# Strassen's scheme for one half of an output projection, on one Trainium2 core

## The chip, the cores and the metric

The kernel runs on one core of a Trainium2 chip. TensorE (PE) multiplies matrices and loads its stationary operand in a sub-stream of its own (PEld); VectorE (DVE), ScalarE (ACT) and GpSimd (POOL) do elementwise work; SyncE (SP) issues nearly all transfers, which run on 16 DMA engines. Each engine takes its instructions in order, and they synchronize by semaphores. The metric is the device time of one execution in microseconds. The kernel before took 450.61 us, the median of three runs (448.91 to 451.24).

## The reference

One encoder layer on 1024 tokens of width 1024: a combined input projection, two groups of attention heads, a gate on each, an output projection, and a LayerNorm over residual and projection.

```python
h = jnp.einsum('bsd,de->bse', x, w_in[layer])
q_a, k_a, v_a, z_a, q_b, k_b, v_b, z_b = jnp.split(h, SPLIT_POINTS, axis=-1)
y_a = neighborhood_attention(...)            # 8 heads, 8 x 16 window on a 16 x 64 grid
y_b = windowed_gqa_with_sink(...)            # 8 query heads, 2 key heads, |i - j| <= 128, rotary
mixed = jnp.concatenate([y_a * jax.nn.silu(z_a), y_b * jax.nn.silu(z_b)], axis=-1)
y = jnp.einsum('bse,ed->bsd', mixed, w_out[layer])
x = layer_norm(DEEPNORM_ALPHA * x + y, ln_gain[layer], ln_bias[layer])
```

All inputs are float32. The change concerns `y = mixed @ w_out`, a 1024 x 1024 x 1024 product, and what prepares its operands.

## The kernel before

**Precision.** Each float32 operand of a large product is split into two float16 parts, h (rounded) and l (the rest), after a scale by a power of two. A product is then three matmuls: h*h, h*l and l*h, added up in PSUM. A split is a cast on ACT (the h part) and, for l, one operation on DVE or two on POOL: scale (`L975`), subtract (`L976`).

**Stages.** First the values and the first six column blocks of the input projection. Then the attention: 128 units (group, head pair, head, block of 128 queries), the 'b' heads first. In one unit PE multiplies queries by keys (`stage_qk`, L799 and L800), DVE adds bias or mask and takes the row minimum of the negated scores (L809), ACT exponentiates (L823), ACT and DVE split the result (L831, L832), a DMA transposes it (L835), and PE multiplies it by the values one group of four units at a time (`stage_pv`, L861), some nine units later. `stage_on` normalizes, `stage_ot` transposes on PE (L882) and multiplies by the gate (L885, L888) into `zt[e]`, one tile of 128 mixed channels by 1024 tokens for each e from 0 to 7. The 'b' heads are e = 4 to 7, and come first.

**What fills PE.** Between these steps PE runs the rest of the input projection (`project`, L381): a list of matmuls is handed out by `pump_to`, so many for each unit (`FILL_AT`, `FILL_N`). The last of that filler, 60 matmuls, belongs to the output projection already (`out_head`).

**What sets the order.** Inside the attention the order on each engine is the order in which a Python loop over units writes it (`manual_schedule`). Work on the side is put into queues of `Op` for act, dve, pool and sp; in each unit `pop` emits a fixed number of those whose predecessors were emitted earlier. After the loop `ordered.close()` ends the manual order, and `final()` is ordered by the scheduler of the framework.

**PSUM.** Eight banks of 128 x 512 float32: two with tag `pj` (groups of the projection), four with `s` (scores), two with `t`. A bank can be written again once its readers are done.

**Output projection.** `mixed` is the stationary operand by tiles of 128 tokens, `wo` the moving one by halves of 512 columns. `out_mms(t, a, ps, es)` (L1008) adds the products of row tile t and column half a over the depth blocks `es` into one bank. `wo` is loaded by pieces of 256 KB, twice for six of them: once to take its size (`wo_scan`), once to split it (`wo_split`). Eight of the 16 pieces are split in the attention, eight in `final()`; the parts of `mixed` are made for e = 4 to 7 in the attention (`m_queue`, L990 and L991), for e = 0 to 3 in `final()` (`m_split`, L915, L916).

**End of the layer.** `residual` (L1054, L1057) adds a bank to the tile of x and collects statistics; `norm` finishes a row tile: aggregate (L1061), square root on ACT (L1063), reciprocal (L1068), then half of the columns on DVE and half on ACT and POOL (L1102 to L1108), and stores. The last half tile is computed in pieces of 256, 128 and 128 columns, and `norm_last` finishes it.

Of the kernel before, what the change touches and what calls it, by code (L numbers as in the profile page):

```python
# [25 lines left out]
MSCALE = 2.0 ** -44  # L26
QSCALE = 2.0 ** -15
LTT, LPP, BH, ND, NA, NX, F1 = 1, 6, 9, 1, 1, 6, 0.2
# [14 lines left out]
WO_TAG = ("wor", "wor", "raw", "raw") + ("wr",) * 5 + ("wor", "wor", "raw", "raw", "raw", "wr", "wr")  # L43
WO_SCAN = ((9, 2), (12, 4), (10, 6), (13, 8), (14, 10), (15, 13))
WO_PREV = {15: ("s", 9), 0: ("s", 10), 1: ("s", 15), 2: ("s", 12), 3: ("s", 13), 11: ("s", 14)}
WO_SCALE = 55
M_AT = [105, 112, 118, 120]
WO_AT = [67, 71, 75, 79, 84, 88, 93, 98]
WO_LD = [16, 22, 19, 25, 36, 39, 42, 45, 48, 112, 116, 28, 130, 130, 130, 130]
# [7 lines left out]
def hybrid_block(ctx, tc, xT, x, wt, wv, wo, bias, sink, gain, lbias, cos, sin, bmask, out):  # L57
# [15 lines left out]
    vd = dram.tile([4, GW, ROWS, 4 * VE], F16, name="vd")  # L73

# [29 lines left out]
    wos = const.tile([128, 1], F32, name="wos")  # L104
    yc = const.tile([128, 1], F32, name="yc")
# [30 lines left out]
    ENG = ("act", "dve", "pool", "sp")  # L136
# [3 lines left out]
    class Op:  # L140
        def __init__(self, eng, fn, deps, prio):
            self.eng, self.fn, self.deps, self.step = eng, fn, [d for d in deps if d is not None], None
            self.prio, self.born, self.lag = prio, clock["step"], 2 if eng == "sp" else 0

        def emit(self):
            self.fn()
            self.step = -1 if clock["step"] is None else clock["step"]

    def enq(eng, fn, *deps, prio=1, after=0):
        op = Op(eng, fn, deps, prio)  # L150
        if clock["step"] is not None:
            queues[eng].append(op)
        elif after:
            events.setdefault(ran[0] + after, []).append(op.emit)
        else:
            op.emit()
        return op

    ran, events = [0], {}

# [7 lines left out]

    def need(*ops):
        for op in ops:  # L170
            if op.step is None:
                need(*op.deps)
                queues[op.eng].remove(op)
                op.emit()
# [10 lines left out]
    def w_split(m):  # L185
# [18 lines left out]
        o = enq("act", hi, load_ops.get(("w", m)), prio=0.5)  # L204
        o = enq("pool", lo, o, prio=0.5)
# [80 lines left out]
    def split_k(p, half, src, dep=None):  # L286
# [4 lines left out]
        for j in range(2):  # L291
# [5 lines left out]
            def dup_(w, j=j, a=a, o=o):  # L297
# [6 lines left out]
            dup = [enq("pool", lambda d=dup_: d("kh"), o1, after=32 if dep else 0),  # L304
                   enq("pool", lambda d=dup_: d("kl"), o2, after=36 if dep else 0)]
# [101 lines left out]
    with ExitStack() as vctx:  # L407
# [26 lines left out]
        def load_wv(k, cuts=(0, 640)):  # L434
# [4 lines left out]
            h = vw.tile([128, 640], F32R, name=f"wvh{k}")  # L439
            l = vw.tile([128, 640], F32R, name=f"wvl{k}")  # L440
# [9 lines left out]
        def first_tiles():  # L450
            xr = vp.tile([128, 512], F32, tag="xr", name="xraw", bufs=4)
            wr = wv_stage(0)
            h = vw.tile([128, 640], F32R, name="wvh0")
            l = vw.tile([128, 640], F32R, name="wvl0")
# [271 lines left out]
    rawp = ctx.enter_context(tc.tile_pool(name="rawp", bufs=3, reuse_waits="tile"))  # L726
    actx = ExitStack()
    tiles["kq"] = actx.enter_context(tc.tile_pool(name="kq", bufs=4, reuse_waits="tile"))
    ap = actx.enter_context(tc.tile_pool(name="ap", bufs=3, reuse_waits="tile"))
    tiles["ap"] = ap  # L730


# [46 lines left out]
    def stage_qk(u):  # L779
# [12 lines left out]
        else:  # L792
# [5 lines left out]
            init = nsk[:, h:h + 1]  # L798
        nc.tensor.matmul(ps[:, :n], q, sl[0], start=True, stop=False)  # L799
# [15 lines left out]
    def stage_exp(u):  # L815
        m = 128 * geom(u)[1] + (u[0] == "b")
        sn, nm = st.pop((u, "sn")), st.pop((u, "nm"))
# [8 lines left out]
    def stage_tr(u):  # L826
        n, m = geom(u)
        pt = st.pop((u, "p"))
        hl = split[units.index(u) % NSPLIT]
        src = pt[:, :128 * m].rearrange("p (k c) -> p k c", c=128)  # L830
# [32 lines left out]
    def stage_on(q):  # L863
        g, p, j, h = quad(q)
        ps = st.pop((q, "o"))
        ri = ap.tile([128, 4], F32, tag="ri", name="ri", bufs=4)
        w = VE if g == "a" else HD
# [6 lines left out]
    def stage_ot(q):  # L874
# [4 lines left out]
        ps = bank("t")  # L879
        o = on.pop((g, p, h))  # L880
# [12 lines left out]
    FILL_N = [48] * len(FILL) + [9, 9, 6, 12, 24]  # L893
# [10 lines left out]
    mh, ml = {}, {}  # L904
    EO = (4, 5, 6, 7, 0, 1, 2, 3)

    def m_alloc(e):
        if e >= 4:
            t = big_tile(f"m{e}", (128, 2, S), F16)
        else:  # L910
            t = tiles["fp"].tile([128, 2, S], F16, tag="m", name=f"m{e}", bufs=4)
        mh[e], ml[e] = t[:, 0, :], t[:, 1, :]

    def m_split(e, sl, hi, lo):
        hi(mh[e][:, sl], zt[e][:, sl])  # L915
        lo(ml[e][:, sl], zt[e][:, sl], mh[e][:, sl])  # L916

    WO_SEQ = [(e, a) for a in range(2) for e in EO[:4]] + [(e, a) for e in EO[4:] for a in range(2)]
    wo_parts = {}

    wo_raw = {}

    def wo_load(n, scan=False):
        tag = ("wor" if n in (9, 10, 15) else "raw") if scan else WO_TAG[n]
        pool, bufs = (rawp, 3) if tag == "raw" else (wp, {"wr": 5, "wor": 2}[tag])
        raw = pool.tile([128, 512], F32, tag=tag, name=f"wor{n}", bufs=bufs)
        e, a = WO_SEQ[n]
        nc.sync.dma_start(raw, wo[e, :, 512 * a:512 * a + 512])
        wo_raw[("s", n) if scan else n] = raw

    wo_ops = {}

    def wo_scan(n, scan=False):
        def act():
            raw = wo_raw.pop(("s", n))
            nc.scalar.activation(raw, raw, AF.Abs, accum_out=wom[:, n:n + 1])

        def dve():
            nc.vector.tensor_reduce(wom[:, n:n + 1], wo_raw[n], axis=mybir.AxisListType.X, op=ALU.add,
                                    apply_absolute_value=True)  # L940

        load = load_ops["wo", ("s", n) if scan else n]
        wo_ops["s", n] = enq("act", act, load) if scan else enq("dve", dve, load)

    def wo_scale():
        need(*[wo_ops["s", n] for n in range(16)])
        ps = bank("t")
        nc.tensor.matmul(ps[:, :16], ones, wom.bitcast(BF16)[:, 1::2], start=True, stop=True)
        nc.vector.tensor_reduce(wog, ps[:, :16], axis=mybir.AxisListType.X, op=ALU.max)
        nc.vector.tensor_scalar_max(wog, wog, 2.0 ** -30)  # L950
        nc.vector.tensor_scalar(wog.bitcast(I32), wog.bitcast(I32), 0x7F800000, None, op0=ALU.bitwise_and)
        nc.vector.tensor_scalar(wos.bitcast(I32), wog.bitcast(I32), 0x7F800000, None, op0=ALU.bitwise_xor)
        nc.vector.tensor_scalar(yc, wog, mc, 1.0, op0=ALU.mult, op1=ALU.mult)

    def wo_split(n):
        def hi():
            if n % 2 == 0:
                if n < 8:
                    t = big_tile(f"wo{n}", (128, 2, 2, 512), F16)
                else:  # L960
                    t = tiles["fp"].tile([128, 2, 2, 512], F16, tag="wo", name=f"wo{n}", bufs=4)
                for i in range(2):
                    wo_parts[n + i] = [t[:, i, 0, :], t[:, i, 1, :]]
            if hi_eng == "act":
                nc.scalar.activation(wo_parts[n][0], wo_raw[n], AF.Copy, scale=wos)
            else:
                nc.vector.tensor_scalar_mul(wo_parts[n][0], wo_raw[n], wos)

        def lo():
            h, l = wo_parts[n]  # L970
            raw = wo_raw.pop(n)
            if q == "dve":
                nc.vector.scalar_tensor_tensor(l, raw, wos, h, op0=ALU.mult, op1=ALU.subtract)
            else:
                nc.gpsimd.tensor_scalar(raw, raw, wos, 1.0, op0=ALU.mult, op1=ALU.mult)  # L975
                nc.gpsimd.tensor_sub(l, raw, h)  # L976

        q = "dve" if n in (2, 5, 8, 9, 10, 11, 14) else "pool"
        hi_eng = "act" if clock["step"] is not None or WO_SEQ[n][1] == 1 else "dve"
        o = enq(hi_eng, hi, load_ops.get(("wo", n)))  # L980
        o = enq(q, lo, o)
        wo_ops[n] = o

    m_ops = {}

    def m_queue(e):
        m_alloc(e)
        m_ops[e] = []
        for h in (slice(0, 512), slice(512, S)):
            o = enq("act", lambda h=h: nc.scalar.copy(mh[e][:, h], zt[e][:, h]))  # L990
            m_ops[e].append(enq("pool", lambda h=h: nc.gpsimd.tensor_sub(  # L991
                ml[e][:, h], zt[e][:, h], mh[e][:, h]), o))
# [5 lines left out]
    def out_mms(t, a, ps, es, c=(0, 512)):  # L998
        o, w = c
        ts, cs = slice(128 * t, 128 * t + 128), slice(o, o + w)  # L1000
        ps = ps[:, o:o + w]
        for e in es:
            n = WO_SEQ.index((e, a))
            if n in wo_ops:
                need(wo_ops[n], *m_ops.get(e, ()))
            woh, wol = wo_parts[n]
            for i, (lh, rh) in enumerate(((mh[e], woh), (mh[e], wol), (ml[e], woh))):
                nc.tensor.matmul(ps, lh[:, ts], rh[:, cs],  # L1008
                                 start=(e == EO[0] and i == 0), stop=(e == EO[-1] and i == 2))
                yield  # L1010
# [14 lines left out]
    def final():  # L1025
# [5 lines left out]
        for e in EO[4:]:  # L1031
            m_alloc(e)
# [268 lines left out]
```

## Time and profile before

| | |
|---|---|
| Median of three runs | 450.61 us |
| Profiled execution | 447.86 us, of which the span of instructions is 446.1 us |
| PE busy | 438.3 us (98%), 3241 matmuls |
| DVE, ACT, POOL busy | 346.8, 302.6, 211.7 us |
| Last matmul of the output projection | about 439.0 us from the start of the span |
| DMA | 71.20 MB, mean 160 GB/s |

In a row of instruction groups the columns are line, engine, operation, out<-in, shape and count, then busy time in us and the mean duration of one in ns, then the idle time of the engine just before them and what ended it. In a row of a chain or a timeline the first number is the start in us from the start of the span, the second the length. A row of waits has the waiting engine and line, the one that released it, then the total in us, how often, and the longest. "DMA to landing", and the last number of a DMA issue, is the time from issue until the data is there. Matmuls overlap, so the distance between two starts says more than the duration of one.

### The profile page before, as it was taken

To read this page: it belongs to the slowest core of one execution; us is meant where nothing else is said; L and a number is where in the kernel's file an instruction comes from. 1 tells how busy PE (TensorE), PEld (TensorE's weight loads), DVE (VectorE), ACT (ScalarE), POOL (GpSimd) and SP (SyncE) were. 2 spreads that over 40 slices of the span, in tenths; PEclk is the share of its full clock that TensorE was granted. 3 is DMA by queue.
4 is the path that set the end of the run, shared out by engine and by line. 5 is a ranking of instruction groups with operands and counts; after the bars stand their busy time and mean duration, and the time that the engine had idled before them with its cause. 6 is when DMAs were issued, how large, how long until landed. Compare 5 with 4: busy or idle time off the path is not lost.

```text
span 446.1 us, 9265 instructions
## 1 busy us (share of the span) xinstructions
PE 438.3 (98%) x3241; PEld 254.7 (57%) x3241; DVE 346.8 (78%) x842; ACT 302.6 (68%) x636; POOL 211.7 (47%) x227
## 2 busy tenths in 40 slices
PE   9999999999999999999999999999999999999995
PEld 8997754444445565655564655555555654444454
DVE  5988867429986797898988887888877737679945
ACT  5849789666599988886867777777777847012411
POOL 0110074636939558767505656655642404304740
PEclk9999999999999999999999999999999999999998
DMA  7921569991149999586876769569569588102711
GB/s 266 391 94 60 164 222 325 278 307 54 48 118 221 188 202 181 95 159 135 168 109 126 144 130 169 112 135 184 116 110 242 108 185 318 48 1 92 238 72 71
DMA packets 123983, 71.20 MB, mean 160 GB/s; under 512 B 96800, under 2 KB 105888, under 8 KB 123936
## 3 DMA queue, kind: packets, MB, share of 16 engines
q1 hardware_dynamic: 123792, 70.48, 65.6%
q8 instruction: 25, 0.41, 0.4%
q14 instruction: 22, 0.18, 0.1%
q10 hardware_dynamic: 144, 0.13, 0.1%
HBM read 41.19 MB, written 6.32 MB: 107 GB/s over the span
## 4 chain that ended last, share of the span: by engine, by line
PE 82%; ACT 5%; DVE 4%; DMA 4%; issue 3%; POOL 1%; SPq 0%; DVEq 0%; POOLq 0%; ACTq 0%
PE ps_pj L381 36%; PE ps_s L1008 9%; PE ps_s L488 6%; PE ps_t L861 6%; PE ps_pj L1008 5%; PE ps_t L1008 5%; PE ps_s L799 3%; PE ps_s L800 3%; PE ps_pj L488 3%; PE ps_t L488 3%; DMA vd<-vt 2%; DMA ws<-in_wt 2%; ACT split L831 1%; PE ps_t L882 1%; DVE qs L257 1%
## 5 line engine op out<-in xcount | busy, mean ns | idle before, releaser
L381 PE MATMUL ps_pj<-xf,wh 128*128 128x512 f16 x672 | 201.3, 379 | 0.9 <-DVE ks L257 0.5
L381 PE MATMUL ps_pj<-xf,wl 128*128 128x512 f16 x336 | 127.3, 379 | 0.0
L381 PEld LDWEIGHTS <-wh 128*128 128x128 f16 x672 | 63.4, 98 | 61.9 <-DVE ks L257 1.3
L823 ACT ACTIVATE ps_s<-sn,nm 128x385 f32<-128x385 f32 (+3 forms) x128 | 70.9, 554 | 29.0 <-DVE nm L809 28.6
L832 DVE SCALAR_TENSOR_TENSOR split<-ps_s,split 128x384 f16<-128x384 f32 (+1 forms) x128 | 66.8, 522 | 30.1 <-ACT split L831 28.4
L1008 PEld LDWEIGHTS <-m 128*128 128x128 f16 x432 | 40.0, 98 | 41.2 <-DVE m L916 0.3
L831 ACT ACTIVATE split<-ps_s 128x384 f16<-128x384 f32 (+1 forms) x128 | 58.6, 458 | 2.4
L381 PEld LDWEIGHTS <-wl 128*128 128x128 f16 x336 | 32.9, 98 | 38.3
L198 POOL TENSOR_SCALAR wr<-wr,wsc 128x512 f32<-128x512 f32 x26 | 20.5, 790 | 66.6 <-ACT wh L193 54.4
L809 DVE CUSTOM_DVE_ANT_0 sn<-ps_s,bm,nsk 128x384 f32<-128x384 f32 (+1 forms) x64 | 40.7, 635 | 0.8 <-PE ps_s L800 0.6
L1008 PE MATMUL ps_s<-wo,m 128*128 128x512 f16 (+1 forms) x192 | 40.7, 366 | 0.0
L799 PE MATMUL ps_s<-ks,qs 128*128 128x384 f16 (+2 forms) x128 | 39.7, 310 | 0.1
L800 PE MATMUL ps_s<-ks,qs 128*128 128x384 f16 (+2 forms) x128 | 39.7, 310 | 0.0
L809 DVE CUSTOM_DVE_ANT_0 sn<-ps_s,bias,sg 128x368 f32<-128x368 f32 (+1 forms) x64 | 36.2, 565 | 3.8 <-PE ps_s L800 3.2
L861 PEld LDWEIGHTS <-tr 128*128 128x128 f16 (+1 forms) x1056 | 36.2, 98 | 2.4
L199 POOL TENSOR_TENSOR wl<-wr,wh 128x512 f16<-128x512 f32 x26 | 32.7, 1256 | 2.2
L299 POOL COPY ks<-ks 64x512 f16<-64x512 f16 x40 | 26.2, 663 | 13.8 <-ACT ks L251 5.2
L1008 PE MATMUL ps_pj<-wo,m 128*128 128x512 f16 (+1 forms) x144 | 26.5, 326 | 0.0
L1107 POOL TENSOR_TENSOR xr<-xr,gb 128x512 f32<-128x512 f32 x7 | 9.8, 1398 | 32.5 <-ACT xr L1104 32.5
L1008 PE MATMUL ps_t<-wo,m 128*128 128x512 f16 x96 | 22.8, 379 | 0.0
L488 PEld LDWEIGHTS <-xf 128*128 128x128 f16 x192 | 18.6, 98 | 7.2
L800 PEld LDWEIGHTS <-qs 128*128 128x128 f16 x128 | 12.5, 98 | 15.5 <-issue 0.8
(190 smaller groups left out, 783.6 us busy)
## 6 DMA issues: line engine op xcount, KB each, us to landing
ws<-in_wt SPq DMA_DIRECT2D x15, 512.0 KB, 6.9
wr<-in_wt SPq DMA_DIRECT2D x26, 256.0 KB, 3.5
wor<-in_wo SPq DMA_DIRECT2D x22, 256.0 KB, 3.3
xr<-in_x SPq DMA_DIRECT2D x8, 512.0 KB, 8.7
out<-xr SPq DMA_DIRECT2D x15, 256.0 KB, 2.0
bias<-in_bias SPq DMA_DIRECT2D x8, 440.0 KB, 3.9
wvraw<-in_wv SPq DMA_DIRECT2D x9, 320.0 KB, 5.8
xraw<-in_xT SPq DMA_DIRECT2D x11, 256.0 KB, 4.4
```

Of the source, the lines that this page charges most:

```text
L199: nc.gpsimd.tensor_sub(l, raw, h)
L299: nc.gpsimd.tensor_copy(place(t, o, half, col), place(t, a, half, col))
L381: nc.tensor.matmul(ps, a[:, k % 4, :], mv, start=(k == 0 and i == 0), stop=(k == KT - 1 and i == 2))
L488: nc.tensor.matmul(ps[:, :320], lh[:, ts], rh[:, cs], start=(k == ko[0] and i == 0), stop=(k == ko[-1] and i == 2))
L799: nc.tensor.matmul(ps[:, :n], q, sl[0], start=True, stop=False)
L800: nc.tensor.matmul(ps[:, :n], q, sl[1], start=False, stop=True)
L809: nc.vector.tensor_tensor_reduce(sn[:, :n], ps[:, :n], bias_t, sg[:, c:c + 1], init, op0=ALU.add, op1=ALU.min, accum_out=nm)
L823: nc.scalar.activation(pt[:, :m], sn[:, :m], AF.Exp, bias=nm, scale=-1.0, accum_out=acc)
L831: nc.scalar.activation(hl[:, :m, 0, :], src, AF.Copy, scale=PSCALE)
L832: nc.vector.scalar_tensor_tensor(hl[:, :m, 1, :], src, PSCALE, hl[:, :m, 0, :], op0=ALU.mult, op1=ALU.subtract)
L861: nc.tensor.matmul(ps[:, w * m:w * m + e], a, b_, start=(i == 0), stop=(i == len(mms) - 1))
L1008: nc.tensor.matmul(ps, lh[:, ts], rh[:, cs], start=(e == EO[0] and i == 0), stop=(e == EO[-1] and i == 2))
```

## The change

The 'b' half of the depth (e = 4 to 7) becomes two pairs of depth blocks. For each pair the product is a 2 x 2 block product: A11, A12, A21, A22 are the halves of 512 tokens by the two depth blocks of `mixed`, B11 to B22 the two depth blocks by column halves of `wo`. Winograd's form of Strassen's scheme computes it with seven block products (q1 to q7 in `TERMS`) instead of eight; it needs four sums S1 to S4 of blocks of `mixed` and four, T1 to T4, of blocks of `wo`. The 'a' half stays as eight. In `final()` row tiles t and 4 + t are worked on together, and a bank is read by DVE and then added into further: q1 goes to C11, with q6 on top to C12, with q7 on top to C22, with p4 on top to C21. So an `add` on DVE stands between matmul groups on the same bank, eight adds for a pair of tiles where there were four.

Around it:

- The sums S are made in float32 in `zt`, the sums T in the loaded tiles of `wo`; then both are split. The split T blocks are stored to DRAM (`td`) and loaded back near the end of the attention.
- `wo` is loaded as four tiles of 1 MB for its size, one of them a second time for the T blocks, and 14 blocks of 256 KB to be split.
- All splits of `wo`, and of `mixed` but for two blocks that depend on the last unit, are in the attention.
- The queues keep books: each step's own work is booked on its engine, an operation may be open to several engines ("any"), and `fill_in` emits one where the planned end of the engine's work lies before the next step.
- `final()` is now inside the manual order; `norm` leaves the columns to ACT and POOL, and four tiles of x are loaded and scaled before it.

```diff
-MSCALE = 2.0 ** -44
+MSCALE = 2.0 ** -46
-    FILL_N = [48] * len(FILL) + [9, 9, 6, 12, 24]
+    FILL_N = [48] * len(FILL) + [12, 12, 6, 15, 18]
...
+    def fill_in(eng):
+        now = at_step(clock["step"])
+        ready = [op for e in (eng, "any") for op in queues[e] if op.prio > 1 and (e == eng or eng in op.cost) and all(
+            d.step is not None and d.step + d.lag < clock["step"] + (d.eng == eng) and (d.eng == eng or d.fin < now)
+            for d in op.deps)]
+        if ready:
+            op = min(ready, key=lambda op: op.prio)
+            queues[op.eng].remove(op)
+            op.emit(eng)
...
+    TERMS = {"q1": [("A11", "B11", n) for n in range(NSP)], "q6": [("S2", "T2", n) for n in range(NSP)],
+             "q5": [("S1", "T1", n) for n in range(NSP)], "q7": [("S3", "T3", n) for n in range(NSP)],
+             "q2": [("A12", "B21", n) for n in range(NSP)] + [(a, b, n) for n in NB for a, b in (("A11", "B11"), ("A12", "B21"))],
+             "q3": [("S4", "B22", n) for n in range(NSP)] + [(a, b, n) for n in NB for a, b in (("A11", "B12"), ("A12", "B22"))],
+             "p4": [("A22", "T4", n) for n in range(NSP)] + [(a, b, n) for n in NB for a, b in (("A21", "B11"), ("A22", "B21"))],
+             "d": [(a, b, n) for n in NB for a, b in (("A21", "B12"), ("A22", "B22"))]}
...
+        for t in range(4):
+            if t == 3:
+                b[3] = run("q1", 3, bank("s"))
+            add(t, 0, b[t])
+            cb = run("q5", t, bank("t" if t < 2 else "s"))
+            run("q6", t, b[t])
+            add(4 + t, 1, cb)
+            if t == 3:
+                add(t, 1, cb)
+            add(t, 1, b[t])
+            if t < 3:
+                run("q2", t, a[t], (5,))
+                add(t, 0, a[t], whole=True)
+            d = run("d", t, bank("pj"))
+            run("q7", t, b[t])
+            add(4 + t, 1, d)
+            add(4 + t, 1, b[t], whole=True)
+            if t < 3:
+                run("q3", t, cb)
+                add(t, 1, cb, whole=True)
+                norm(t)
+            run("p4", t, b[t])
+            add(4 + t, 0, b[t], whole=True)
+            norm(4 + t)
+            for n in ((2, 6), (3, 7), (), ())[t]:
+                x_scale(n)
+        add(3, 0, run("q2", 3, bank("pj")), whole=True)
...
+        if i in T_RD:
+            t_soon((3, 0, 1, 2)[T_RD.index(i)])
+        if i in X_RD:
+            x_soon((0, 4, 1, 5)[X_RD.index(i)])
...
     clock["step"] = None
+    final()
     ordered.close()
-    final()
```

`prod(name, t, ps, ...)` takes the place of `out_mms` and issues three matmuls for each term; `add` takes the place of `residual`.

504 lines of the change are left out of this document (297 added, 207 removed).

## The prediction

> **What bounds the kernel now.** I read the page first, then busy time by stage, then who waits for whom, then the chain that ends last.
>
> ```profile
> span 446.1 us, 9265 instructions
> PE 438.3 (98%) x3241; PEld 254.7 (57%) x3241; DVE 346.8 (78%) x842; ACT 302.6 (68%) x636; POOL 211.7 (47%) x227
> ```
> ```profile
> 122.00:240.00 118.00, 118.00 (x1015) 66.67 (x1014) 99.61 (x282) 97.83 (x249) 72.98 (x73) 1.00 0.81 157
> 240.00:330.00 90.00, 89.01 (x783) 50.74 (x779) 74.13 (x198) 68.85 (x141) 54.66 (x67) 1.00 0.72 136
> 330.00:371.40 41.40, 41.40 (x382) 24.21 (x381) 26.36 (x77) 28.91 (x57) 8.93 (x8) 1.00 0.87 185
> ```
> ```profile
> 371.40:439.00 67.60, 67.60 (x363) 33.27 (x361) 52.66 (x92) 18.44 (x26) 29.09 (x21) 1.00 0.31 113
> ```
>
> Columns of the stages are busy time (and instructions) of PE, PEld, DVE, ACT, POOL, then clock, DMA share, GB/s. The first three are the attention, the fourth the output stage. A busy PE could still be a slow one, so I look at its pace in the chain:
>
> ```profile
> 241.93 0.71 DVE ks L257
> 242.68 1.47 PE ps_pj L381 x6
> ...
> 326.48 0.70 DVE qs L257
> 327.23 0.82 PE ps_pj L381 x3
> ...
> 402.63 5.18 PE ps_t L1008 x24
> ```
>
> 24 matmuls of 512 columns in 5.18 us are 0.216 us each, and the output stage runs at that pace without a hole: matmuls taken out there come off the time one for one, and each new PE wait goes on. In the attention PE loses little, but the rows at 241.93 and 326.48 show it released by a DVE evacuation. There DVE and ACT are nearly as tight as PE (waits from 245 to 325 us):
>
> ```profile
> DVE split L832 <- ACT split L831: 11.0, 19, 0.8
> ACT ps_s L823 <- DVE nm L809: 7.8, 12, 1.1
> ACT qs L251 <- DVE qs L257: 6.0, 6, 1.1
> ACT ks L251 <- DVE ks L257: 4.2, 5, 0.9
> PEld L381 <- DVE ks L257: 0.6, 1, 0.6
> ```
>
> In this stretch DVE and ACT wait for each other and never for PE: both run behind PE and set when PSUM banks come free.
>
> **The change, part by part.** (a) *Matmuls.* Before, the output projection is 8 row tiles x 2 column halves x 8 depth blocks x 3 = 384 products of 512 columns. After, the half of the 'b' heads is 7 products x 2 pairs x 4 tiles x 3 = 168 in place of 192; the other half stays 192. 24 fewer x 0.216 = **-5.2 us**. The last half tile is cut in 256, 128 and 128 columns in both kernels; its share is equal within 0.2 us. In the instruction order 63 of the products lie ahead of the last attention transpose, before it was 72; that only moves the border.
>
> (b) *Hand-offs in the output stage.* Before, a bank is filled once, read once, and PE goes on in another. After, q1's bank is read by DVE, then PE adds q6 into the same bank, DVE reads, q7, DVE reads, p4. PE therefore waits for DVE adds (`add`, one scalar_tensor_tensor each), and this part is now written by hand order. Prices, by form in the output stage:
>
> ```profile
> L1057 DVE BATCH_NORM_STATS2 stats<-xr 128x6 f32<-128x512 f32 x14 | 9.5, 684 | 0.1
> L1054 DVE SCALAR_TENSOR_TENSOR xr<-ps_s,yc,xr 128x512 f32<-128x512 f32 x7 | 5.2, 737 | 5.4 <-PE ps_s L1008 5.4
> L1061 DVE BATCH_NORM_AGGREGATE mv<-stats 128x2 f32<-128x12 f32 x7 | 1.4, 196 | 0.1
> L1068 DVE RECIPROCAL rstd<-sd 128x1 f32<-128x1 f32 x8 | 1.2, 144 | 0.0
> L888 DVE SCALAR_TENSOR_TENSOR z<-ps_t,zc,z 128x512 f32<-128x512 f32 x1 | 0.8, 751 | 3.0 <-PE ps_t L882 3.0
> L1029 DVE MEMSET eps<- 128x1 f32 x1 | 0.1, 59 | 0.0
> ```
> ```profile
> 402.67 0.19 DVE L1061 BATCH_NORM_AGGREGATE mv<-stats 128x2 f32<-128x12 f32 x1
> 402.89 0.29 ACT L1063 ACTIVATE sd<-mv,eps 128x1 f32<-128x1 f32 x1 [2.26 <-DVE mv L1061]
> 436.17 2.84 PE L1008 MATMUL ps_pj<-wo,m 128*128 128x128 f16 x48
> 436.37 0.48 DVE L1054 SCALAR_TENSOR_TENSOR xr<-ps_s,yc,xr 128x256 f32<-128x256 f32 x1 [0.91 <-PE ps_s L1008]
> ```
>
> DVE starts 0.20 us after PE has gone to the next bank (436.17 to 436.37); PE starts 0.04 us after a DVE read (241.93 + 0.71 to 242.68); DVE to ACT and back takes 0.03 to 0.05.
>
> - q6(1) and q6(2): DVE's order between p4 of the tile before and the add that frees q1's bank is add, bn_stats, aggregate, [sqrt on ACT], reciprocal, add: 0.20 + 0.74 + 0.68 + 0.04 + 0.20 + 0.03 + 0.29 + 0.05 + 0.14 + 0.74 + 0.04 = 3.15 us. PE has only q5 meanwhile, 6 x 0.216 = 1.29. Wait 1.86 each, 3.7 together.
> - q6(3): the same chain, but q1(3) and q5(3) cover 2.59: 0.6.
> - q6(0): after the last attention transpose z, the eps memset and the add: 0.20 + 0.75 + 0.06 + 0.74 + 0.04 = 1.79 against 1.29: 0.5.
> - d(0): the pj banks both hold q2 sums begun in the attention, so d(0) waits until q2(0) is read. Two adds after q6(0), 0.20 + 2 x 0.74 + 0.04 = 1.72, less q2's three matmuls 0.65: 1.1.
> - p4(3): q3 was put last, so nothing lies between q7(3) and p4(3): 0.20 + 0.74 + 0.04 = 1.0.
>
> Sum **+6.9 us**. The other reuses have 12 to 18 matmuls (2.6 to 3.9 us) between and cost nothing; without that cover each is again 1.0. Without the 0.24 of hand-off in each of the six it is 5.4; with as much again, 8.3. Behind a waiting PE only its own queue hangs: ACT and DVE have idle time here, and POOL, which now does gain and bias of whole tiles where it did halves, goes from 29.09 us to at most 58 of some 70. The stage's final 7 us (last matmul to the end) do not change.
>
> (c) *Splitting in the attention.* By the order of instructions ACT gets 14 more casts of wo, 12 more of the gated output, and 3 more scans; DVE loses 3 scans and gains some 5 sums or splits, which is even; POOL gains 13 two-step splits, 11 subtracts, 14 sums.
>
> ```profile
> L965 ACT ACTIVATE wo<-wor,wos 128x512 f16<-128x512 f32 x12 | 8.6, 713 | 6.0 <-DMA wor<-in_wo 5.5 <-DMA tr<-split 0.5
> L990 ACT CAST m<-z 128x512 f16<-128x512 f32 x8 | 4.5, 608 | 0.0
> L936 ACT ACTIVATE wor<-wor 128x512 f32<-128x512 f32 x6 | 3.7, 620 | 0.0
> ```
> ```profile
> L976 POOL TENSOR_TENSOR wo<-wor,wo 128x512 f16<-128x512 f32 x6 | 7.0, 1160 | 0.5
> L975 POOL TENSOR_SCALAR wor<-wor,wos 128x512 f32<-128x512 f32 x6 | 4.7, 786 | 0.4
> ```
>
> ACT: 14 x 0.71 + 12 x 0.61 + 3 x 0.62 = 19.1 us on 195.6 of 249.4, 86%. POOL: 13 x 1.95 + 25 x 1.16 = 54 on 136.6, 77%, and no wait of PE on POOL is listed. Room there is, but in order: of ACT's new casts, 6 of wo and 6 of the output (7.9 us) stand among the units that ran from 240 to 330 us. From below this is -1.0, if the new order also ends the waits that PE has there (90.00 less 89.01); from above all 7.9 go on the path. DVE waits for ACT in 11.0 of 80 us, 14%; an ACT cast put there delays DVE by its whole length. 0.14 x 7.9 = **+1.1 us**.
>
> (d) *DMA.* wo was 22 loads of 256 KB. After: five of 1 MB, 14 of 256 KB, 8 stores and 4 loads (512 KB) of the combined blocks, and four x loads move ahead of the end of the attention, all on SP's queue among the transposes. Between the last five transposes stand five 512 KB loads, 2.6 MB.
>
> ```profile
> tr<-split SPq DMA_TRANSPOSE x1, 2.5
> ```
> ```profile
> 358.03 4.46 SPq L835 DMA_TRANSPOSE tr<-split  x3
> 362.54 2.00 SPq L928 DMA_DIRECT2D wor<-in_wo  x4
> ```
> ```profile
> 366.69 1.19 PE L861 MATMUL ps_t<-va,tr 128*128 128x65 f16 x33
> ```
> ```profile
> 352.40:366.20 13.80, 13.80 (x125) 7.68 (x123) 7.02 (x22) 8.51 (x17) 0.00 (x0) 1.00 0.79 148
> 370.00:375.00 5.00, 5.00 (x27) 2.53 (x25) 3.41 (x8) 4.24 (x8) 1.36 (x1) 1.00 1.02 416
> ```
>
> The last transpose is issued 1.2 us before SP's load at 362.54, about 361.3, and lands in 2.5. Loads reached 416 GB/s, so 2.6 MB take 6.3 us; with a DMA share of 0.79 there is room for some 1.7 us of it in the 8 us: the transpose lands 4.6 later, 368.4. PE needs it in the last quarter of the group at 366.69, some 367.4, and by its new order 5 matmuls (1.1) earlier, 366.3: **+2.0 us**; 0 if the queues interleave in its favour, 4.6 if all of it shows. The 1 MB loads cost 2.5 us of queue each, in place of loads that go; they can add up to 1 us at one early group, in the range alone.
>
> [...]
>
> **Sum.** -5.2 + 6.9 + 1.1 + 2.0 = +4.8. The profiled execution took 447.86 us (span 446.1), so 452.7; it was 2.75 under the median of the three timed runs, 450.61, and on that scale it is 455.4. Within 0.5% (2.25 us) a run of this kernel can't be told from no change.
>
> **Rivals.** *Faster: the hand-offs are shorter.* The matmuls win if (b), (c) and (d) together stay under 2.9 us. That would be so if DVE could answer at the tile ends without the square root's round trip in front of the add (0.4 in place of 1.86 at q6(1) and q6(2), nothing at q6(3): (b) 3.4) and (c) stood at its lower end: -5.2 + 3.4 - 1.0 = -2.8, 447.8. For it: DVE is 22% idle in the output stage. Against: DVE's order has the add behind the reciprocal. 0.11.
>
> *No change: attention and DMA take all the extra work.* (a) + (b) = +1.7, 452.3. For it: ACT 14% idle, transposes elsewhere with several us to spare. 0.23.
>
> *Slower by much: ACT and DVE become the bound.* All 7.9 us of (c) and 4.6 of (d): +14.2 with (a) and (b), 464.8; with half of (c) and (d), 458.6. For it: in 245 to 325 us they already never wait for PE. Against: DVE gets no more work. 0.2.
>
> The forecast has the rest, 0.46; its own range is 453 to 458. For 8 in 10 I go from 449, which leaves most of the faster case out, to 463. Faster 0.11, within 0.5% 0.24, slower 0.65. That the matmuls aren't removed is excluded by the instruction order: 36 fewer, 24 and 12 narrow ones.
>
> **What would show it.** (a) 360 products in place of 384. (b) PE gaps of nearly 2 us ahead of q6(1) and q6(2), near 1 at d(0) and p4(3), released by the add's line. (c) ACT near 86% in the attention, PE gaps released by DVE evacuations. (d) the last transposes landing after 5 us or more, and a gap before the last PV group. Wrong if PE runs through the output stage without gaps, or if the attention's gaps sum to over 8 us.

## The result, and the profile after

The changed kernel takes 478.2 us (median of four runs) where the kernel before takes 450.2 beside it: a ratio of 1.062, 95% interval 1.058 to 1.066. The forecast was 455.4 us, 449 to 463. The profiled execution took 477.5 us. From its page, the busy times and the granted clock in 40 slices:

```profile
span 475.6 us, 9303 instructions
...
PE 442.4 (93%) x3205; PEld 253.3 (53%) x3205; DVE 339.0 (71%) x826; ACT 313.6 (66%) x658; POOL 275.8 (58%) x292
...
PEclk9999999999999999999998999998999999999998
```

PE has 36 matmuls less, as planned, and is busy 93% of the span instead of 98%. The busy time by stage, columns as in the prediction (clock third from the end):

```profile
237.00:256.00 19.00, 15.28 (x122) 7.82 (x120) 14.98 (x40) 13.53 (x33) 14.82 (x15) 0.91 1.08 227
256.00:301.00 45.00, 44.86 (x402) 25.95 (x400) 35.40 (x92) 35.19 (x71) 38.05 (x44) 1.00 0.85 162
301.00:327.00 26.00, 19.26 (x135) 9.60 (x133) 16.89 (x42) 16.59 (x34) 17.97 (x20) 0.87 0.77 146
327.00:385.00 58.00, 58.00 (x523) 33.70 (x522) 44.04 (x119) 45.97 (x93) 42.67 (x43) 1.00 0.79 168
385.00:400.00 15.00, 10.40 (x71) 5.39 (x70) 4.79 (x9) 5.81 (x7) 2.27 (x2) 0.89 1.06 385
400.00:466.90 66.90, 61.84 (x319) 29.82 (x319) 36.68 (x70) 14.10 (x18) 34.95 (x33) 1.00 0.17 67
```

Between 256 and 301 us and between 327 and 385 PE is as full as before. Most of the time is lost in three places: 3.7 us of idle PE in the first row, 6.7 in the third, 4.6 in the fifth, and in the same three rows the granted clock is below 1. (Ahead of these rows, from 122 to 198 us, PE is idle for another 2.9 us; 2.2 of them are one wait, the third row of the next list.) DVE is busy 79, 65 and 32% of them, and 79 and 76% of the full stretches beside them; ACT and POOL give no other picture. What PE waited for in the attention, by the list of waits of the changed kernel from 122 to 400 us:

```profile
PE ps_t L916 <- DMA tr<-split: 11.0, 8, 3.3
PE ps_s L851 <- DVE split L887: 3.4, 4, 0.9
PE ps_t L775 <- DVE z L942: 2.2, 1, 2.2
```

In the kernel before, the same view has 0.9 us in all, on the evacuations of the projection. Now the largest is the values' product (L916) waiting for a transposed tile. What held the transposes up at 302 to 316 us is in SP's own order, here its timeline and then its waits at that place:

```profile
302.43 0.57 SPq L823 DMA_DIRECT2D bias<-in_bias  x1
303.10 0.41 SPq L1052 DMA_DIRECT2D wob<-in_wo  x1
303.61 1.19 SPq L890 DMA_TRANSPOSE tr<-split  x1
313.15 0.33 SPq L1052 DMA_DIRECT2D wob<-in_wo  x1
313.59 1.22 SPq L890 DMA_TRANSPOSE tr<-split  x1
```

```profile
SPq L1052 <- DVE wo L996: 8.3, 1, 8.3
```

SP stands for 8.3 us in front of a load of a block of `wo` (L1052), whose buffer is freed by DVE's low half of an earlier block (L996). The next three transposes, whose data are ready at 307.9, 309.7 and 311.5 us, stand behind that load. It is not the transfers that are slow there: what the DMA engines moved from 302 to 316 us, in 40 slices, is nothing for nearly 7 us.

```profile
GB/s 160 162 274 239 125 64 161 221 362 403 377 348 280 96 23 0 0 0 0 0 0 0 0 0 0 0 0 0 0 0 0 0 0 0 64 176 156 198 147 166
```

To compare kernels I add up, over all matmuls, the distance from one start to the next less what the same form takes where nothing waits (0.216 us for 512 columns); distances of 0.40 to 0.43 us between matmuls of 512 columns (0.30 to 0.31 for the scores) count as half clock (from 250.67 to 254.08 us, at a granted clock of 0.50, they are 0.43 and 0.31). "Projection" is from the first score product to the last matmul of the input projection, "tail" from there to the last transposition on PE, "output" the rest. In us:

| | projection | of it half clock | tail | of it half clock | output |
|---|---|---|---|---|---|
| before | 2.5 | 0 | 0.1 | 0 | 2.6 |
| after | 22.5 | 3.9 | 5.7 | 1.3 | 9.7 |

Against the profiled execution of before the span grew by 29.5 us: -5.2 by 24 matmuls, +7.0 of gaps in the output stage, +20.1 and +5.6 in projection and tail, and 1.7 at the very end, where ACT takes 2.06 us to issue the last store and 0.37 before (some of the kernels below have that and others not; I have no reading of it). That is 29.2 of the 29.5.

### The profile page after: what moved, and what is told of

Its sections match the earlier page's. It is cut to its first block, busy times and chain, and to the rows that moved or that the text cites. A ratio compares the mean times of both kernels' runs of the same rounds, so it can differ in the third digit from the quotient of the medians.

```text
span 475.6 us, 9303 instructions
## 1 busy us (share of the span) xinstructions
PE 442.4 (93%) x3205; PEld 253.3 (53%) x3205; DVE 339.0 (71%) x826; ACT 313.6 (66%) x658; POOL 275.8 (58%) x292
## 4 chain that ended last, share of the span: by engine, by line
PE 59%; DVE 10%; ACT 9%; issue 9%; DMA 6%; POOL 6%; SPq 0%; DVEq 0%; ACTq 0%; POOLq 0%
PE ps_pj L421 22%; PE ps_s L1146 9%; PE ps_s L528 6%; PE ps_pj L1146 5%; PE ps_t L916 4%; DMA tr<-split 3%; PE ps_pj L528 3%; PE ps_t L528 3%; ACT split L886 3%; PE ps_s L851 2%; PE ps_s L852 2%; PE ps_t L1146 2%; POOL wl L239 2%; DVE split L887 2%; DVE qs L297 2%
## 5 line engine op out<-in xcount | busy, mean ns | idle before, releaser
L421 PE MATMUL ps_pj<-xf,wh 128*128 128x512 f16 x672 | 203.8, 383 | 0.3 <-DVE qs L297 0.3
L421 PE MATMUL ps_pj<-xf,wl 128*128 128x512 f16 x336 | 128.7, 383 | 0.0
L916 PEld LDWEIGHTS <-tr 128*128 128x128 f16 (+1 forms) x1056 | 37.2, 98 | 14.5 <-DMA tr<-split 12.1
L1146 PEld LDWEIGHTS <-m 128*128 128x128 f16 x234 | 22.4, 99 | 30.6 <-issue 8.2
L1193 ACT ACTIVATE sd<-mv,eps 128x1 f32<-128x1 f32 x8 | 2.4, 294 | 41.7 <-DVE mv L1191 41.7
L916 PE MATMUL ps_t<-va,tr 128*128 128x65 f16 (+1 forms) x528 | 20.7, 195 | 8.3 <-DMA tr<-split 8.3
L1181 DVE SCALAR_TENSOR_TENSOR xr<-ps_s,yc,xr 128x512 f32<-128x512 f32 (+1 forms) x22 | 15.7, 729 | 15.8 <-PE ps_s L1146 15.8
L1146 PE MATMUL ps_s<-T,m 128*128 128x512 f16 x84 | 20.4, 379 | 5.1 <-DVE xr L1181 5.1
L1085 POOL TENSOR_TENSOR m<-z,m 128x512 f16<-128x512 f32 x15 | 17.1, 1162 | 13.7 <-ACT m L1082 13.6
L1242 POOL TENSOR_TENSOR xr<-xr,gb 128x512 f32<-128x512 f32 x13 | 16.5, 1271 | 13.2 <-ACT xr L1240 8.1
```

The costliest lines, as they stand in the source:

```text
L421: nc.tensor.matmul(ps, a[:, k % 4, :], mv, start=(k == 0 and i == 0), stop=(k == KT - 1 and i == 2))
L916: nc.tensor.matmul(ps[:, w * m:w * m + e], a, b_, start=(i == 0), stop=(i == len(mms) - 1))
L1146: nc.tensor.matmul(ps[:, cs], lh[:, 128 * t:128 * t + 128], rh[:, cs], start=(fresh and e == 0 and n == 0), stop=(e == len(terms) - 1 and ...
```

## The experiments

Three theories. **A**: SP's order and the bulk transfers make the transposes late. **B**: DVE and POOL have too much to do for the splits and sums. **C**, formed when e4 to e7 had left gaps of 10 us: the pieces put into ACT's order delay the attention's own splits. (The first expectations counted ACT among the engines of B as well.) Times are medians, with the ratio to the kernel before run beside them (448.1 to 449.4 us). The changed kernel's 478.2 us stood beside 450.2, so a difference of medians against it holds 1 to 2 us by which the sets of runs differ; the ratios don't.

**e1: loads later.** In `b_split`:

```diff
         b_ops[n] = enq("any", lambda eng: lo_of(...), o, prio=1.8, cost=LOW)
+        b_ops[n].lag = 6
```

> Only the loads of the 'a' heads' blocks of wo that reuse a staging buffer change: each is handed to SP's queue six steps later than its buffer's last reader was planned. In the changed kernel SP stood 8.3 us in front of one of them (for a DVE split of block 4), with three transposes of the attention behind it, and TensorE lost about 10.7 us between 302 and 326 us. Theory A (SP's in-order queue and the bulk transfers make the transposes late): the 8.3 us wait goes, the gaps there shrink to about 1 us, and the time falls from 478.2 to about 468.5 us (466 to 471). Theory B (ACT, DVE and POOL have too much to do for the splits, and the load's wait is only where it shows): the same work is still to be done in the same place, and the time stays at 476 to 480 us.

471.5 us, 1.050. In 296 to 330 us the load's wait has gone:

```profile
SPq L1052 <- POOL bias L826: 0.5, 1, 0.5
```

The gaps of the projection fell from 22.5 to 17.8 us; those of 302 to 326 us from 10.7 to 3.6, half a dozen short ones that are left. A holds, for about two thirds of that place; the time is just above the 466 to 471 us expected.

**e2: quarters.** `wo_load` and `wo_scan`:

```diff
-            nc.sync.dma_start(wor[i], wo[i])
+            nc.sync.dma_start(wor[i][:, b], wo[i, :, b])
...
+        for b in range(4):
+            load_ops["wor", i, b] = load_ops["wor", i] = enq("sp", lambda b=b: load(b), *deps)
```

> Only the 1 MB loads of wo in the attention change: each is issued as four loads of 256 KB, at most one in each step. Theory A, its part on transfers: the transposes issued next to a 1 MB load landed after 5.6 to 8.4 us where others take 2.5 to 4; with quarters they land after 5 us at the most, the three waits of the PV products between 246 and 249 us (3.2 us) and the half clock behind them (1.7 us) go, and the time falls by 4 to 6 us, to about 473 us. Theory B: the number of bytes and the work of the engines are the same, the gaps stay, 476 to 480 us. If the SP queue's own issue time (15 more loads of 0.4 to 0.6 us) counts instead, it is slower than 480 us.

472.4 us, 1.052. The transposes issued between 236 and 250 us (the last number is us to landing), after and then here:

```profile
wor<-in_wo SPq DMA_DIRECT2D x1, 1024.0 KB, 8.3
wob<-in_wo SPq DMA_DIRECT2D x4, 256.0 KB, 5.1
...
tr<-split SPq DMA_TRANSPOSE x6, 5.9
```

```profile
tr<-split SPq DMA_TRANSPOSE x8, 4.3
```

The waits of that place went: for transposes PE waits 0.3 us in all from 122 to 365 us. So did the stall at 302 us, where the later splits came in another order, and the start of the output stage got worse by 5 us (2.6 of them for the add of x). The net gain agrees with A, its place only in part.

**e3: loads behind.** All of T's and four of x's loads behind the last transposes:

```diff
-T_RD = [124, 126, 128, 130]
-X_RD = [125, 127, 129, 131]
+T_RD = [129, 130, 131, 132]
+X_RD = [129, 130, 131, 132]
```

> Only the loads of T and of four x tiles change: they are issued behind the attention's last transposes instead of among them. Theory A: units 125 to 127's transposes land after 2.5 to 4 us instead of 4.6 to 6.4, the three waits between 386 and 391 us (4.2 us) and the half clock behind them (2.8 us in all) go, and the time falls by about 7 us, to 471 us (469 to 473), unless the first sixth product now waits for its T. Theory B: nothing of this place is due to the loads, 476 to 480 us.

482.3 us, 1.074: a miss. The last transposes were in time (tail 0.1 us), but the output stage lost 20.0 us. ACT's scaling of x now stands in its order, waiting for the later loads, ahead of the last split that PE needs:

```profile
ACT xr L1044 <- DMA xr<-in_x: 13.1, 4, 8.3
```

**e4: the three together**, and the scale of `wo` later:

```diff
-        if scans and ... op.fin < at_step(i) for op in scans):
+        if scans and ... op.fin + 4 < at_step(i) for op in scans):
```

> The three edits together, and the scale of wo taken 4 us of planned time later (TensorE waited 2.4 us for it at 191 us). Theory A: the gaps of the attention fall from about 26 us to 3, the hand-offs of the output stage stay at 7.0 us, and the time is about 455 us (452 to 459), the 455.4 us of the prediction. Theory B: the splits need engines that are not there; the gaps come up in other places, and the time stays above 468 us.

468.2 us, 1.042 (1.038 to 1.045). Projection 10.2 us, tail 0.1, output 20.9. The long stalls of the attention are gone, and PE meets the same wait behind x as in e3 (5.6 us, and 2.0 for T). The time alone is at the edge of what B expected (above 468), but its largest wait is again a load's place in a queue, not an engine that lacks time. What the 10.2 us are stayed open.

**e5: the add first.** The output stage alone, in `final()`:

```diff
-            add(t, 0, b[t])
+            if t in (0, 3):
+                add(t, 0, b[t])
             cb = run("q5", t, bank("t" if t < 2 else "s"))
...
+            if t < 2:
+                add(t + 1, 0, b[t + 1])
             run("p4", t, b[t])
```

> Against the changed kernel only the output stage's order on DVE: the first add of row tiles 1 and 2 (which empties the bank that the sixth product goes on filling) stands ahead of the adds and the row statistics of the tile before, in a stretch where DVE is idle. If the two waits of 1.86 and 1.99 us before these sixth products are DVE's order, as the prediction has it, both go to under 0.3 us and the time falls by 3.5 us, to about 474.7 us. If the bank comes free late for another reason, the waits stay and the time is 478 us.

472.1 us, 1.052. PE's waits in the output stage, of the changed kernel and then of e5:

```profile
PE ps_s L1146 <- DVE xr L1181: 4.9, 4, 1.8
PE ps_t L1218 <- ACT dr L1216: 1.9, 1, 1.9
PE ps_pj L1146 <- DVE xr L1181: 0.9, 1, 0.9
```

```profile
PE ps_t L1218 <- ACT dr L1216: 1.9, 1, 1.9
PE ps_s L1146 <- DVE xr L1181: 1.4, 2, 0.8
PE ps_pj L1146 <- DVE xr L1181: 0.9, 1, 0.9
```

Both waits ahead of q6(1) and q6(2) went; the stage's gaps fell from 9.7 to 5.9 us, by 3.8, where the prediction had put 3.7 on DVE's order. The rest of the 6 us is not this edit's: the gaps of projection and tail together are as before (28.0 us, 28.2 before), and the kernel before, run beside them, differs by 1.9 us itself (450.2 and 448.3).

**e6: all so far, and the end rearranged.** e1, e2, e5, the later scale, and

```diff
-T_RD = [124, 126, 128, 130]
-X_RD = [125, 127, 129, 131]
+T_RD = [124, 125, 127, 129]
+X_RD = [128, 131, 132, 133]
...
         m_last()
+        for t in (0, 4, 1, 5):
+            x_scale(t)
```

(T in the order 0, 3, 1, 2, and no scaling of x in `x_soon`.)

> The edits of e1, e2 and e5 and the later scale, and at the end of the attention T's four loads among the last transposes in the order in which the products need them, the loads of x behind, and ACT's scaling of x behind the last split of the attention's result (in e3 and e4 ACT stood in front of it waiting for x, and TensorE waited 3.9 and 5.6 us for that split). Theory A with ACT's queue added: the end of the attention and the first block of the output stage lose 3 to 5 us instead of 13, the two hand-offs 3.5 us less, and the time is 455 us (452 to 460), so no faster than before. Theory B: what is cured at one place comes up at the next, over 464 us.

462.6 us, 1.031 (1.028 to 1.035). Better than e4, but projection 9.9 us, tail 5.1, output 8.1. The time lies between the two expectations, 7.6 us above the 455 of theory A, and neither theory says what the 9.9 are.

**e7: less work for DVE and POOL.** As e6, but

```diff
-            return enq("any", lambda eng: on_eng[eng].tensor_sub(wor[i][:, o], ...), ...)
+            return load_ops["wor", i]
...
-        b_ops[n] = enq("any", lambda eng: lo_of(part[key][1], b_raw.pop(n), ...), ...)
+        b_ops[n] = o
```

and the sums S likewise. This kernel leaves out the 16 sums and the low halves of 14 blocks of `wo`, so what it computes is no longer the layer; only its time is of use.

> As e6, but without the 16 sums and differences of Strassen's scheme and without the low halves of the fourteen 'a' blocks of wo (their high half is used twice): 30 pieces of work of DVE and POOL less, every transfer and every product as in e6. It asks what the gaps of 10 us that e4 kept in the attention's projection part are. Theory A (transfers and queues): they stay, and the time is within 2 us of e6. Theory B (DVE and POOL busy with the splits): they fall to the 2.5 us of the kernel before, and the time is 6 to 8 us under e6.

464.6 us, 1.035: no faster than e6, projection 10.6 us, with POOL at 154 us instead of 187 in 122 to 371 us. B falls for POOL: 30 fewer instructions there gain nothing. Of DVE's 552 instructions in that stretch only 4 went (200.7 to 198.5 us), so e7 says nothing about DVE; but DVE has no more to do after the change than before it (339.0 us busy in the whole span, 346.8 before).

**e8: T earlier, x behind.**

```diff
-T_RD = [124, 125, 127, 129]
-X_RD = [128, 131, 132, 133]
+T_RD = [120, 121, 122, 123]
+X_RD = [129, 131, 132, 133]
...
+        x_scale(0)
         m_last()
-        for t in (0, 4, 1, 5):
+        for t in (4, 1, 5):
```

> As e6, but T's four loads are issued four steps earlier, right behind the last projection, x's four behind the last transpose, and the first x is scaled ahead of the last split. In e6 the transposes of units 123 to 127 still landed after 4.4 to 6.3 us beside T's loads (two waits of 1.5 and 1.8 us and 1.7 us of half clock), and the first bank of the output stage waited 2.5 us for the scaled x. Theory A: these 7 us go, and the time is 455.5 us (453.5 to 458). If the loads' bytes and not their place count, the waits move to the units before, and it stays at 461 to 464 us.

460.0 us, 1.025 (1.021 to 1.029). 2.6 of the 7 us: tail 3.1 instead of 5.1, output 6.5 instead of 8.1. The waits moved to the transposes of units 119, 122 and 123, which now lie beside T's loads (landing after 5.9 to 7.7 us). The place of the waits is that of the second expectation; the time, 460.0, lies between the two.

**e9: high halves on POOL.** As e8, but in `t_prep` and `b_split`

```diff
-            nc.scalar.activation(part[key][0], b_raw[n], AF.Copy, scale=wsn)
+            nc.gpsimd.tensor_scalar(part[key][0], b_raw[n], wsn, 1.0, op0=ALU.mult, op1=ALU.mult)
...
-        o = enq("act", hi, load_ops["wo", n], *deps, prio=1.8, cost=0.65)
+        o = enq("pool", hi, load_ops["wo", n], *deps, prio=1.8, cost=0.8)
```

> As e8, but the 22 high halves of wo's blocks (8 of T, 14 of the 'a' heads) are made on POOL and not on ACT. It asks again for the gaps of about 10 us in the projection part, which e7 left as they were. Theory C: each of these pieces on ACT stands in ACT's order ahead of a split of the attention, and DVE's low half, the transpose and the bank behind it come later (DVE waited 28.4 us for ACT's splits in the kernel before, 41.3 after, 39.5 in e7); then that wait falls to about 30 us, the gaps fall to 4 us, and the time is 5 us under e8. If ACT's order is not it, the time is that of e8 or, with POOL at 85% of the attention, a few us more.

456.2 us, 1.013 (1.007 to 1.019). DVE's wait for ACT's splits in 122 to 365 us: before, after, e9.

```profile
DVE split L832 <- ACT split L831: 28.4, 48, 1.3
```

```profile
DVE split L887 <- ACT split L886: 41.3, 57, 2.8
```

```profile
DVE split L887 <- ACT split L886: 28.2, 47, 2.2
```

It is back at the value of before, and the time falls by 3.8 us. The projection's gaps fall from 10.1 to 7.2 us, not to the 4 expected, and 1.3 us come up in the tail. C holds, with less than the 5 us expected.

**e10: halves of T.** As e9, T's loads as eight of 256 KB from step 119 to 126, and

```diff
-            d = run("d", t, bank("pj"))
+            d = run("d", t, bank("pj" if t else "t"))
```

> As e9, but T's four loads of 512 KB are eight of 256 KB, one a step from the last projection on, and the first product of the lower right block goes into the other pair of banks (it waited 1.6 us for the add that empties its own). In e9 the transposes of units 120 to 123 landed after 6.1 to 8.3 us beside T's loads, and TensorE waited 2.0 and 1.1 us for them. Theory A: they land after 5 us or less, these waits, the half clock behind them (0.6 us) and the 1.6 us go, and the time is about 451 us (449 to 454), level with the kernel before. If the bytes and not the size of one load count, only the 1.6 us go, 454.5 us.

453.1 us, 1.010 (1.006 to 1.015). From 358 (356) to 372 us, e9 and then e10:

```profile
T<-td SPq DMA_DIRECT2D x3, 512.0 KB, 6.8
tr<-split SPq DMA_TRANSPOSE x7, 6.1
```

```profile
T<-td SPq DMA_DIRECT2D x6, 256.0 KB, 4.2
...
tr<-split SPq DMA_TRANSPOSE x9, 4.1
```

With the same bytes in loads of half the size the transposes land 2 us earlier. Both kernels issue one of these loads a unit (`T_RD`), so the bytes are spread over twice as many units as well, and no run tells size from rate. Of the two waits of 2.0 and 1.1 us behind them one of 1.9 stays; the half clock (the mean granted clock of the profiled execution is 0.992 in e9 and 0.996 here) and the 1.6 us at d(0) are gone. Projection 6.5 us, tail 3.0, output 4.9. The intervals of e9's and e10's ratios overlap, so the gain shows in these waits and not yet in the time. This is the best version of the scheme that I ran, and it still is 3.8 us behind the kernel before.

**e11: POOL alone.** The edit of e9 on the changed kernel, nothing else.

> The changed kernel with one edit alone: the 22 high halves of wo's blocks on POOL instead of ACT, all loads and waits as they were. If ACT's order were what makes the attention's splits and so the transposes late at all places (theory C alone), the three long stalls would shrink and the time would be under 466 us. If SP's queue and the transfers are (theory A with C as a second cause of some 4 us), the three stalls stay and the time is 473 to 476 us.

465.1 us, 1.035 (1.029 to 1.041): 13.1 us by one edit that touches no load (12 by the ratios, from two executions). Two of the three stalls shrank, projection 22.5 to 10.2 us, the third (the tail, 5.1) stayed. SP's wait at 296 to 330 us, 8.3 before:

```profile
SPq L1052 <- DVE wo L996: 1.0, 1, 1.0
```

Neither expectation fits as it stands. The cast, the low half behind it, the load that waits for the low half's buffer and the transposes behind the load are one chain; e1 cuts it at its third link, e11 at its first.

**e12: ACT's pieces in the kernel before.**

```diff
         nc.scalar.activation(pt[:, :m], sn[:, :m], AF.Exp, ...)
+        for _ in range(PIECES.count(units.index(u))):
+            nc.scalar.activation(idle_out, identf.unsqueeze(1).to_broadcast([128, 4, 128]), AF.Copy, scale=0.25)
```

> The kernel before with one thing added: 22 pieces of work on ACT (128x512 to fp16, as a high half of wo's blocks takes; their output is used by nobody), each in ACT's order behind the same attention split as the 22 in the changed kernel. Nothing else of the change is in it: no Strassen products, no further loads, no further work of DVE or POOL. Theory C by itself (a piece ahead of a split delays the transposes, whatever else runs): 13 us more as e11 gave back, 455 to 463 us. If the pieces cost so much only through what hangs on them in the changed kernel (the low half behind each, the load that waits for that half's buffer at the head of SP's queue, the transposes behind that load): within 2 us of the kernel before.

455.8 us where the kernel before takes 448.1: 1.016 (1.012 to 1.020).

```profile
L828 ACT ACTIVATE idle_out<-identf 128x512 f16<-128x512 f32 x22 | 13.6, 618 | 0.1
```

```profile
PE ps_s L801 <- DVE split L836: 2.2, 5, 0.7
PE ps_pj L383 <- DVE qs L259: 2.2, 2, 1.9
PE ps_pj L383 <- DVE ks L259: 0.8, 3, 0.3
PE ps_t L865 <- DMA tr<-split: 0.6, 2, 0.4
```

The gaps of the projection go from 2.5 to 10.7 us, by some twenty short ones (0.2 to 0.8 us, one of 2.1), with no long wait for a transpose and nothing lost in tail or output. DVE's wait for ACT's splits in 122 to 365 us rises from 28.4 to 35.3 us. So the pieces cost 7.7 us by themselves, for 13.6 us of work on an engine that is idle a fifth of the time there. The time is at the lower end of the first expectation, short of its 13 us: the other 4 to 5 us of e11's gain would be what hangs on the pieces in the changed kernel. That is a difference of two runs, with some 4 us to either side, and the match is rough: this kernel has its own casts of `wo` besides, and eight of the pieces stand right ahead of one of them.

The gaps of all runs in us (half clock included) and the median time:

| | projection | tail | output | time |
|---|---|---|---|---|
| e1 | 17.8 | 5.5 | 10.2 | 471.5 |
| e2 | 14.3 | 5.5 | 15.0 | 472.4 |
| e3 | 21.1 | 0.1 | 20.0 | 482.3 |
| e4 | 10.2 | 0.1 | 20.9 | 468.2 |
| e5 | 21.2 | 6.8 | 5.9 | 472.1 |
| e6 | 9.9 | 5.1 | 8.1 | 462.6 |
| e7 | 10.6 | 6.1 | 8.1 | 464.6 |
| e8 | 10.1 | 3.1 | 6.5 | 460.0 |
| e9 | 7.2 | 4.4 | 6.5 | 456.2 |
| e10 | 6.5 | 3.0 | 4.9 | 453.1 |
| e11 | 10.2 | 5.1 | 10.2 | 465.1 |
| e12 | 10.7 | 0.1 | 2.6 | 455.8 |

## Why the prediction was wrong

The direction was right, the size not: of +28 us it had +4.8. The attention (projection and tail) lost 25.6 us more than before, where (c) and (d) had 3.1.

**(a), right.** 36 matmuls less, 24 of them of 512 columns.

**(b), right, its wait by wait too.** Predicted and measured gaps in us: q6(1) 1.86 and 1.86, q6(2) 1.86 and 1.99, q6(3) 0.6 and 0.71, q6(0) 0.5 and 0.38, d(0) 1.1 and 1.02, p4(3) 1.0 and 1.00; sum 6.9 and 7.0. e5 took the cause away, and the two largest went with it. Counting an engine's instructions between the read that frees a bank and the one ahead of it gave these numbers to a tenth.

**(c), wrong: +1.1 us, of at most 7.9.** The step that failed is "0.14 x 7.9", the share of time in which DVE waits for ACT, times the casts put between 240 and 330 us. 22 pieces of that kind cost 7.7 us in the kernel before (e12), 0.35 us for each, and taking the changed kernel's 22 off ACT gave 13.1 (e11). Neither is the term itself: the change adds 14 of these casts and 12 of the gated output. At 0.35 us each, as an estimate, these 26 are 9.1 us. The share of idle time was no measure: the chain of cast on ACT, low half on DVE, transpose and bank is serial with little slack. In the trace of the changed kernel 19 of the 22 casts stand directly ahead of a split of the attention, which begins without a gap behind the cast, and in the 4 us behind a cast ACT is idle for 1.0 us on average, more than the 0.71 of the cast: the split waits and ACT idles a little later. e7 and e9 point to the same: 30 pieces off POOL gave nothing, and 22 off ACT gave 3.8 us although POOL took them over. No run leaves the casts on ACT and moves them to other places, so that it is their place and not their amount rests on this trace and not on an experiment.

**(d), wrong: +2.0 us.** Two steps. "Up to 1 us at one early group, in the range alone" was for the 1 MB loads; it is 3.2 us of waits at 246 to 250 us. And the loads were priced by their bytes alone. That a load itself waits, for a buffer that an engine frees, and holds everything behind it on SP, stands in no term: the 8.3 us at 304. The last group's wait, "+2.0" (2.1 by its own figures), is 4.2 in the trace, on the transposes of units 125 to 127. In e8 and e9 the wait followed T's loads to the units that came to lie behind them (2.4 and 2.7 us for transposes after 365 us, by the lists of waits); whether these transposes stood behind the loads or shared the bandwidth with them, no run tells.

**Left out: the clock.** It has no term. 5.2 of the 28 us are matmuls at half clock behind the stalls (below). The sentence "Wrong if ... the attention's gaps sum to over 8 us" names what happened.

**The rivals.** "Slower by much" had a chance of 0.2 and came nearest, with 464.8 still 13 us short. It named ACT and DVE as the bound. DVE's work did not grow (339.0 us busy, 346.8 before), and what cost was work in the order of ACT, and of SP, which it leaves out. "The matmuls win" is not excluded as such: e10 gets the hand-offs to 2.2 us, but its attention still loses 7 us more than that of before.

**Open.** How the 9.5 us that e10 still loses in projection and tail divide between ACT's order and the transfers. By its list of waits 4.0 us are for transposes and 2.2 for banks that DVE empties; the rest is in gaps too short for the list. How the 25.6 us divide between (c) and (d) is open as well: e1 and e11 cut the same chain, so their gains can't be added.

## What to carry to other kernels

In an in-order queue, look at what each instruction waits for, not at how busy its engine is: a load that waits for a buffer holds the latency-critical transfers behind it (8.3 us on SP here), and a short cast ahead of a due one costs its place in the chain (22 of 0.62 us cost 7.7 us in e12). Where transfers with a deadline share a queue with bulk loads, keep the bulk loads small, one for each step (4.1 us to landing for 6.1 from e9 to e10), and issue them only when their buffer is free (gaps of 3.6 us for 10.7 in e1). Hand-offs between two engines on a serial path can be predicted to a tenth of a microsecond by counting (6.9 us predicted here, 7.0 measured); loss by order can't be read from average idle time, so bound it by the whole length of the work moved, and more where other queues hang on it. Look at the granted clock behind short gaps too: in the changed kernel three of 1.0 to 1.2 us close together were followed by 3.4 us at 0.50.

## What the hardware showed that I hadn't expected

**Half clock after short gaps.** Windows of the changed kernel around the waits of 246 to 250 us:

```profile
249.50:250.70 1.20, 0.86 (x12) 0.57 (x13) 1.11 (x7) 0.93 (x3) 1.12 (x3) 0.99 1.15 314
250.90:253.90 3.00, 3.00 (x9) 1.15 (x8) 2.30 (x5) 1.66 (x4) 2.84 (x3) 0.50 1.42 153
254.00:258.00 4.00, 4.00 (x21) 1.99 (x20) 2.63 (x8) 2.92 (x6) 2.02 (x3) 0.99 0.91 255
```

PE is 100% busy in the window at 0.50: a page that shows PE busy doesn't show this. Three gaps of 1.0 to 1.2 us within 4 us of each other were followed by 3.4 us at half clock, which begin at 250.67 us; PE busy is the first number behind the comma:

```profile
247.26:250.67 3.41, 1.58 (x30) 1.08 (x29) 2.69 (x10) 2.64 (x8) 3.19 (x5) 1.00 1.19 331
250.67:254.08 3.41, 3.41 (x11) 1.29 (x9) 2.71 (x6) 2.07 (x4) 3.25 (x3) 0.50 1.31 151
```

Other gaps with as much idle PE were not followed by it. The wait at 191 us, here first in the changed kernel and then in e1, left PE idle for 2.1 and 2.2 us; behind it the clock is 1.00 in the one and 0.50 in the other:

```profile
191.40:193.90 2.50, 0.39 (x2) 0.00 (x0) 2.35 (x6) 2.50 (x8) 2.35 (x3) 1.00 0.86 133
194.00:198.00 4.00, 3.99 (x22) 2.09 (x23) 3.83 (x17) 1.87 (x6) 2.74 (x3) 1.00 0.38 84
```

```profile
192.00:194.60 2.60, 0.38 (x3) 0.01 (x1) 2.47 (x6) 2.60 (x9) 2.37 (x4) 1.00 1.01 129
195.40:198.60 3.20, 3.20 (x10) 1.36 (x9) 3.10 (x14) 1.20 (x3) 1.95 (x3) 0.50 0.46 103
```

Nor were the hand-off waits of 1.86 and 1.99 us in the changed kernel followed by it: the clock is 1.00 from 400 to 466.9 us. What decides between them is open. In the changed kernel the clock was at 0.50 four times: from 250.67 us for 3.41 us, from 318.94 for 6.83, from 390.62 for 3.41, and from 472.54 to the end. The first three cost 5.2 us (3.9 and 1.3 in the table of gaps), a third of the 15.0 us in which PE was idle at these places (3.7, 6.7 and 4.6).

**Bulk loads beside a transpose.** The same 2 MB of T in 256 KB instead of 512 KB loads, one a unit in both, brought the median landing of the transposes among them from 6.1 to 4.1 us (e9, e10), and the transposes issued right behind 1 MB loads in the changed kernel landed after 5.6 to 8.4 us. Whether the size of a load or the bytes in a given time do it, no run here tells.
